# The opening of a one-layer decoder: zeros before the first rows, rows in half loads, a third tile's rows in a weight's place, and a new order where queries, keys and the feed-forward start

## The chip, the cores and the metric

The kernel runs on one core of one Trainium2 chip. A core has several engines that each work through their own instructions in order: TensorE (PE in the profile; its weight loads are PEld), VectorE (DVE), ScalarE (ACT), GpSimd (POOL) and SyncE (SP), which here issues the transfers (DMAs) between the memory of the device and the memory beside the engines. The engines wait for one another by semaphores. The metric is the device time of one execution in microseconds (us). The kernel before takes 2188.39 us, the median of 3 runs (2185.43 to 2188.78).

## The reference

One layer of a decoder, for a prompt of 2048 tokens and 64 sample tokens (8 sequences of 8), width 1024, all in 32-bit floats. Cut to what matters here:

```python
h = rms_norm(x, g_mix_pre)
proj = jnp.einsum('btd,de->bte', h, w_in)
q, k, v, gq, gk, gv, gr, glr = jnp.split(proj, points, axis=-1)
q, k = rope(q, pos), rope(k, pos)
attn = swa_banded(q, k, v, sinks)        # window of 128 tokens, 8 query heads, 2 key heads of 64
log_a = log_sigmoid(glr @ w_gk2 + b_gk) / 16
o, s_new = gla_chunked(gq, gk, gv, log_a, s_init)
gla_out = rms_norm(o, g_gla) * silu(gr)
x = x + rms_norm(concat([attn, gla_out]) @ w_out, g_mix_post)
u = relu(rms_norm(x, g_ffn_pre) @ w_up)  # 1024 -> 4096
x = x + rms_norm((u * u) @ w_down, g_ffn_post)
```

The sample tokens go through the same layer with a cache of keys and values and a state of the gated attention. Returned are the two outputs, the last windows of keys and values, and the states.

## The kernel before

**Numbers.** TensorE multiplies in a reduced 32-bit form, so each operand is split into a high part (written by ACT) and a low part (what is left, by DVE: source less high part), and each product is three: high by high, high by low, low by high. A name that ends in `h` or `_hi` is a high part, in `l` or `_lo` a low part. A helper class, `InOrder`, keeps the instructions that are recorded through `te`, `ac` and `dv` (TensorE, ScalarE, VectorE) in the order of the code; all of those carry line L131 in the profile. What goes through `nc.gpsimd` and `nc.sync` stands on POOL and SP in the order of the code as well. Nothing is put in order at run time.

**Stages.** The tokens are cut into tiles of 128 rows, 16 of the prompt and one of the samples.

1. *Opening* (`start`). The rows of tiles 0 and 1 (`x_0`, `x_1`) are loaded, turned by TensorE (`xT`: eight products of 128x128 with the identity, in two halves) and split (`xh`, `xl`). The 784 columns of `w_in` that make q, k, v and the gate's ranks come in 16 pieces (`wa_raw`) and are split too (`wa_hi`, `wa_lo`), with the gain column `gcol`. Then come the first column half of the projection for both tiles, the second half for tile 0, tile 2's rows in between, the second half for tile 1, and the first queries and keys.
2. *Attention* (loop `for i in range(NB)`). For each tile four units of scores (`sc`), turned probabilities (`pT`) and values (`av`). In between TensorE fills in the projection of later tiles (`fill`). A table, `A_PLAN`, says at which unit and phase the side work is done: the row norm of tile i+3 (`junk`, then `rstd`), the rotation of tile i+1, its turned queries and keys (`pq`, `pk`, in `heads_T`), and their splits (`qh`, `ql`, `kh`, `kl`; in the code `hi1`, `lo0`, `lo1`, `klo0`, `klo1`). From i = 3 on two pieces of the gate's weights (`wg`) are loaded and split per tile. At i = 4 in the code, `load_consts` makes the masks and `wgk`; those of its instructions that are not kept in order by the helper stand wherever their inputs and the scheduler put them.
3. *Gated attention*, then the *output projection* with the row norms that follow.
4. *Feed-forward*. The up projection is done with seven products for eight (sums of blocks, `H[p]` for the tokens' sums and `s13`, `s24` for the weights' sums). The tokens' sums are built per pair of tiles in a tile `ht` of seven rows and stored (`h_d`). The first block column is special (`opening(p, ...)`): its products are worked in the order `UP_FIRST` = 1, 0, 2, 8, 5, 7, 9, 6, 3, 4, where 0, 8 and 9 are steps of the sample tokens, and the last rows of the stage before are finished between them. The results (`uX`, `uc`, `ud`, `ue`, `ua`, `ub` in the profile, by the bank they lie in) are added into `st`.

**Where a transfer waits.** SP's transfers take eight semaphores in rotation; a tile that is written again waits until the readers of its old content are done, and a reader may be a store that has not landed.

Of the kernel before, what the change touches and what calls it, by code (L numbers as in the profile page):

```python
# [21 lines left out]
P = 128  # L22
# [34 lines left out]
A_LEAD = 14  # L57
A_PLAN = [(name, (int(at[0]), at[1])) for name, at in dict(
    klo0="3T", first="1B", hi1="3C", x1="1B", lo1="0A", klo1="0B", rest="3A", lo0="3A", junk="2A", turn="1A", rstd="1A", vl="3S", x0="1A"
# [57 lines left out]
def f32(ap):  # L117
    return ap.bitcast(F32)
# [23 lines left out]
def hybrid_step_kernel(ctx: ExitStack, tc: tile.TileContext, I, O):  # L142
# [100 lines left out]
    with nc.allow_non_contiguous_dma(reason="a column of gains"):  # L243
        nc.sync.dma_start(gcol, I["g_mix_pre"][0].rearrange("(k p) -> p k", p=P))

# [38 lines left out]
    def load_x(i):  # L284
        xs_in[i] = x = sp.tile([P, D], F32, tag="x", name=f"x_{i}", bufs=2)
        nc.sync.dma_start(x[: rows(i)], x_rows(i))
# [125 lines left out]
    def heads_T(i):  # L412
# [12 lines left out]
        pk = bank([P, P], "b", f"pk_{i}")  # L425
# [12 lines left out]
        for r in range(2):  # L438
# [10 lines left out]
        def k_lo(r):  # L449
            dv.tensor_tensor(kl[half_of[r], r, 1, :], pk[half_of[r]], f32(ks[half_of[r], r, 1, :]), op=ALU.subtract)  # L450
            nc.gpsimd.tensor_copy(kl[half_of[1 - r], r, 1, :], f32(kl[half_of[r], r, 1, :]))

        def q_lo(r):
# [4 lines left out]
        return {  # L458
            "klo0": lambda: k_lo(0),
# [182 lines left out]
    def load_consts():  # L642
# [12 lines left out]
        for u, rr in enumerate(half_of):  # L655
            nc.scalar.activation(wgk[rr, u], gk[rr], AF.Copy)
            lo = slice(u * HD + 32, u * HD + HD)
            nc.vector.tensor_tensor(gk[lo], gk[lo], f32(wgk[lo, u]), op=ALU.subtract)
            nc.vector.tensor_tensor(wgk[lo, u], gk[lo], extra[lo], op=ALU.add)
        at = [0]  # L660

        def part(n, shape, dtype):
# [3 lines left out]
            nc.vector.tensor_copy(t.rearrange("p a b -> p (a b)") if len(shape) > 1 else t, src)  # L666
# [9 lines left out]
        return wgk, msk, smsk, dmsk, onehot, ggla  # L676
# [9 lines left out]
    def start():  # L686
# [16 lines left out]
        load_x(0)  # L703
# [3 lines left out]
        load_x(1)  # L707
# [23 lines left out]
        for k in range(KT):  # L731
            split(1, k)
            run(second[0], 3)
        for norm in norms:
            norm()
# [1529 lines left out]
```

## Time and profile before

| what | number |
|---|---|
| median of 3 runs | 2188.39 us (2185.43 to 2188.78) |
| the profiled execution | 2189.12 us, its span 2187.3 us |
| TensorE busy | 2156.4 us, 99% of the span |
| DVE, ACT, POOL busy | 1530.3, 1221.7, 251.7 us |
| transfers | 411.54 MB, mean 188 GB/s |
| mean granted TensorE clock | 0.995 of full |

The span is the profiled part of one execution; the execution's own time is 1.8 us longer. In the lists of waits and of instructions a row names the tile that is written and the tiles that are read (`out<-in`), and in square brackets the time for which the engine was idle before it and what it had waited for. "PEclk" is the granted clock as a share of the full one. Matmuls overlap their successors, so the time from start to start of two rows is what TensorE needs, and the duration that a row shows is somewhat longer.

### The profile page before, as it was taken

The numbers are of one execution on the slowest core, as the hardware profiler recorded it, in microseconds if no ns is written. First come the engines' busy times: TensorE is split into PE (matmuls) and PEld (weight loads), VectorE is DVE, ScalarE is ACT, GpSimd is POOL, SyncE is SP. The second block draws the span as 40 slices with busy tenths as digits, with TensorE's granted clock in tenths as the row PEclk, the third lists the DMA queues.
The fourth block names the chain that finished last, engine by engine and source line by source line (L and its number), as shares of the span: only waits on it lengthen the run. The fifth ranks groups of instructions, "written<-read, shape, count | busy, mean of one in ns | idle before, by whom it ended". The sixth has DMA issues, their size and how long they took to land.

```text
span 2187.3 us, 34212 instructions
## 1 busy us (share of the span) xinstructions
PE 2156.4 (99%) x11784; PEld 1866.2 (85%) x11784; DVE 1530.3 (70%) x3203; ACT 1221.7 (56%) x2626; POOL 251.7 (12%) x410
## 2 busy tenths in 40 slices
PE   8999999999999999899999999999999999999998
PEld 7999999999998888788888887888888888888886
DVE  5999968777775666788888555548676666555566
ACT  5899867566663544555555544435444455444444
POOL 2567521111121100000000000000000000000000
PEclk9999999999999999999999999999999999999999
DMA  6444331224337666777876777758544443766685
GB/s 223 139 138 158 103 116 60 69 84 157 108 137 261 216 202 212 233 261 250 276 251 244 255 237 221 242 180 269 182 179 151 159 142 128 238 203 196 194 270 185
DMA packets 240314, 411.54 MB, mean 188 GB/s; under 512 B 25924, under 2 KB 142124, under 8 KB 236028
## 3 DMA queue, kind: packets, MB, share of 16 engines
q1 hardware_dynamic: 240140, 409.35, 56.5%
q8 instruction: 93, 1.52, 0.3%
q14 instruction: 81, 0.66, 0.1%
HBM read 265.82 MB, written 143.99 MB: 187 GB/s over the span
## 4 chain that ended last, share of the span: by engine, by line
PE 92%; DVE 3%; ACT 2%; DMA 1%; issue 1%; POOL 0%; SPq 0%; DVEq 0%; ACTq 0%; POOLq 0%
PE dn L131 27%; PE gproj L131 12%; PE uc L131 8%; PE uX L131 8%; PE out L1335 7%; PE proj L131 6%; PE ud L131 4%; PE ub L131 4%; PE ue L131 4%; PE sam L131 1%; PE dsam L131 1%; PE sc L131 1%; PE pT L131 1%; PE o L131 1%; PE av L131 1%; PE out L131 1%
## 5 line engine op out<-in xcount | busy, mean ns | idle before, releaser
L131 PE MATMUL dn<-o0t,o0s 128*128 128x512 f32 x896 | 349.3, 390 | 2.9 <-ACT o0t L219 1.3
L131 PE MATMUL dn<-o1t,o0s 128*128 128x512 f32 x896 | 349.6, 390 | 0.7 <-DVE o1t L220 0.7
L131 PE MATMUL dn<-o0t,o1s 128*128 128x512 f32 x896 | 349.3, 390 | 0.0
L220 DVE TENSOR_TENSOR o1s<-rs,o0s 128x512 fp32r<-128x512 f32 x224 | 154.6, 691 | 231.4 <-ACT o0s L219 226.6
L219 ACT ACTIVATE o0s<-rs 128x512 fp32r<-128x512 f32 x224 | 141.1, 631 | 305.4 <-PE dn L131 286.1
L131 PE MATMUL gproj<-wg,gxh 128*128 128x384 f32 x1024 | 272.6, 342 | 0.0
L131 PEld LDWEIGHTS dn<-o0t,o0s 128*128 128x128 f32 x896 | 168.2, 188 | 40.4 <-ACT o0t L219 2.1
L131 PEld LDWEIGHTS dn<-o1t,o0s 128*128 128x128 f32 x896 | 168.2, 188 | 37.9 <-DVE o1t L220 2.1
L131 PEld LDWEIGHTS dn<-o0t,o1s 128*128 128x128 f32 x896 | 168.2, 188 | 35.2
L131 ACT ACTIVATE st<-st 128x512 f32<-128x512 f32 x224 | 141.2, 630 | 99.6 <-DVE st L131 94.4
L131 PE MATMUL uc<-H,s 128*128 128x512 f32 x768 | 188.9, 395 | 2.8 <-ACT st L131 2.8
L131 PEld LDWEIGHTS gproj<-wg,gxh 128*128 128x128 f32 x1024 | 183.7, 188 | 3.5 <-issue 3.1
L131 PE MATMUL gproj<-wg,gxl 128*128 128x384 f32 x576 | 185.6, 340 | 0.0
L131 PE MATMUL uX<-H,w 128*128 128x512 f32 x768 | 185.6, 390 | 0.0
L131 PEld LDWEIGHTS uc<-H,s 128*128 128x128 f32 x768 | 144.6, 190 | 33.9 <-ACT st L131 3.0
L131 PEld LDWEIGHTS uX<-H,w 128*128 128x128 f32 x768 | 144.4, 188 | 30.6
L220 DVE TENSOR_TENSOR o1t<-rt,o0t 128x512 fp32r<-128x512 f32 x224 | 153.1, 684 | 9.4 <-ACT o0t L219 9.2
L1335 PE MATMUL out<-wo,mt 128*128 128x512 f32 x680 | 158.6, 392 | 0.0
L209 POOL TENSOR_TENSOR frs<-rs_v,half 128x1 f32<-128x1 f32 (+1 forms) x13 | 10.1, 786 | 1211.6 <-DVE rs_v L207 690.2
L1335 PEld LDWEIGHTS out<-wo,mt 128*128 128x128 f32 x680 | 126.5, 188 | 26.1
L219 ACT ACTIVATE o0t<-rt 128x512 fp32r<-128x512 f32 x224 | 138.1, 617 | 12.0 <-DMA rt<-t_d 8.8
L131 DVE TENSOR_TENSOR st<-st 128x512 f32<-128x512 f32 x160 | 110.6, 691 | 29.2 <-ACT st L131 25.0
(407 smaller groups left out, 4300.2 us busy)
## 6 DMA issues: line engine op xcount, KB each, us to landing
s_d<-st SPq DMA_DIRECT2D x32, 1792.0 KB, 8.5
rs<-s_d SPq DMA_DIRECT2D x224, 256.0 KB, 2.8
raw<-in_w_up SPq DMA_DIRECT2D x64, 512.0 KB, 4.4
rt<-t_d SPq DMA_DIRECT2D x128, 256.0 KB, 3.8
rt<-in_w_down SPq DMA_DIRECT2D x96, 256.0 KB, 3.2
t<-in_w_down SPq DMA_DIRECT2D x64, 256.0 KB, 3.9
t_d<-t SPq DMA_DIRECT2D x32, 512.0 KB, 3.2
hraw<-h_d SPq DMA_DIRECT2D x20, 512.0 KB, 4.9
```

Of the source, the lines that this page charges most:

```text
L131: ins = call(*a, **k)
L209: nc.gpsimd.tensor_tensor(out, v[:n], e, op=ALU.pow)
L219: nc.scalar.activation(hi, src, AF.Copy)
L220: vector.tensor_tensor(lo, src, f32(hi), op=ALU.subtract)
L1335: te.matmul(banks[c], x, w[:, c * 512 : (c + 1) * 512], start=k + u == 0, stop=k == KT - 1 and u == len(products) - 1,)
```

## The change

There are five parts.

1. *Zeros first.* TensorE multiplies a 128x128 tile of zeros by itself 16 times before anything else. The rows of tile 0 are loaded in two halves of their columns, the gain column's load moves behind them, the rotation tables (`rope`) of tiles 0 to 2 move behind the weights, and tile 2's rows are loaded earlier. The row norms of tiles 0 and 1 are done within the second column half's loop, and the stores of their turned rows are issued before that loop.
2. *Tile 2's rows* lie in the place of gate weight 1 (free until i = 3), so that splitting them no longer waits for the stores of tile 0's.
3. *First queries and keys first.* For tile 0 the turned keys get a bank of their own ("c"), the splits of its queries and keys stand ahead of tile 1's remaining columns, half of the key copies moves into the first unit, the row norm of tile 2 moves behind the first unit's scores, and DVE instead of POOL makes the second copies of `kl`. `A_OPEN` is a small table for what is left of this at i = 0.
4. *Constants and gate weights.* The arithmetic of `load_consts` becomes a step of the table (i = 4, unit 2, phase A) and half of it goes from DVE to POOL. At i = 3 the two gate weights are split at two units instead of one; at i = 15 the additional one moves from unit 2 to unit 3.
5. *Feed-forward opening.* The rows of tile 11 are copied to `ht` one step earlier; the second half of the tokens uses one `ht` tile for all four pairs, and its rows 0 and 1 are stored by themselves, ahead of the other five; the two loads of `H41`, `H40` change places; the additions, squares and splits around products 6, 3 and 4 change order; the low part of the next weight and the sum `s24` move; the last additions of the first block column move ahead of the next one's.

```diff
+    (name, (int(at[0]), at[1]))
+    for name, at in dict(kh1="0T", norm2="0S", rs2="0C").items()
+WARM = 16
...
-        nc.sync.dma_start(gcol, I["g_mix_pre"][0].rearrange("(k p) -> p k", p=P))
...
-        pk = bank([P, P], "b", f"pk_{i}")
+        pk = bank([P, P], "b" if i else "c", f"pk_{i}")
...
+        k_hi(0)
         if i > 0:
+            k_hi(1)
...
-            nc.gpsimd.tensor_copy(kl[half_of[1 - r], r, 1, :], f32(kl[half_of[r], r, 1, :]))
+            if i > 0:
+                nc.gpsimd.tensor_copy(kl[half_of[1 - r], r, 1, :], f32(kl[half_of[r], r, 1, :]))
+            else:
+                dv.tensor_tensor(kl[half_of[1 - r], r, 1, :], pk[half_of[r]], hi, op=ALU.subtract)
...
-            nc.scalar.activation(wgk[rr, u], gk[rr], AF.Copy)
-            lo = slice(u * HD + 32, u * HD + HD)
-            nc.vector.tensor_tensor(gk[lo], gk[lo], f32(wgk[lo, u]), op=ALU.subtract)
-            nc.vector.tensor_tensor(wgk[lo, u], gk[lo], extra[lo], op=ALU.add)
...
+        def make():
+            for u, rr in enumerate(half_of):
+                ac.activation(wgk[rr, u], gk[rr], AF.Copy)
+                lo = slice(u * HD + 32, u * HD + HD)
+                nc.gpsimd.tensor_tensor(gk[lo], gk[lo], f32(wgk[lo, u]), op=ALU.subtract)
+                nc.gpsimd.tensor_tensor(wgk[lo, u], gk[lo], extra[lo], op=ALU.add)
+            for copy in made:
+                dv.tensor_copy(*copy)
...
-        load_x(0)
+        warm = sp.tile([P, 2 * P], F32, tag="spc", name="warm", bufs=2)
+        nc.vector.memset(warm[:, :P], 0.0)
+        idle = bank([P, P], "e", "idle")
+        for _ in range(WARM):
+            te.matmul(idle, warm[:, :P], warm[:, :P], start=True, stop=True)
+        load_x(0, 2, rope=False)
...
-        for norm in norms:
-            norm()
+        load_x(2, rope=False)
+        for i in range(3):
+            load_rope(i)
...
+        store()
+        for k in range(KT):
+            split(1, k)
+            run(second[0], 3)
+            if k in (1, 3):
+                norms[k // 2]()
+        xTs[2] = [t[:, :, :P] for t in gw[G_EARLY[1]][1:]]
...
+        left = heads_T(0)
+        for name in ("hi1", "klo0", "lo0", "lo1"):
+            left.pop(name)()
         rest = take_rest(1)
         rest()
-        norm = x_norm(2)
         load_x(3)
-        store()
-        for left in heads_T(0).values():
-            left()
-        norm()
+        left["norm2"] = lambda: left.update(rs2=x_norm(2))
...
-                split_some(2)
+                split_some(1 if i == 3 else 2)
...
-                split_some(1 + (u == 2))
+                split_some(1 + (u == 3))
+            elif u == 2 and i == 3:
+                split_some(1)
...
+            for u in ((1, 0) if (sb, p) == (0, 4) else (0, 1))
...
-            sums[sb, j] = ht_place(f"ht_{i}")
+            sums[sb, j] = sums[sb, j - 1] if sb and j else ht_place(f"ht_{i}")
...
+            if i < NB and sb and i != B_ORDER[-2]:
+                nc.sync.dma_start(h_d[sb][:, :2, :, q], ht[:, :2])
             return
...
-        latest_store[:] = [nc.sync.dma_start(h_d[sb][:, kept, :, q], ht[:, kept])]
+        latest_store[:] = [nc.sync.dma_start(h_d[sb][:, 2:, :, q], ht[:, 2:])]
...
+def split_low(sb, fc, which, vector):
+        hi, lo = halves_[sb, fc, which]
+        vector.tensor_tensor(lo, raws[sb, fc][which], f32(hi), op=ALU.subtract)
...
-                deque(before, 0)
+                if fc > 1 or sb:
+                    deque(before, 0)
...
+            elif p == 5:
+                deque(before, 0)
...
         if p == 1:
+            for copy in late_copies:
+                ac.activation(*copy)
+            nc.sync.dma_start(h_d[1][:, :2, :, 3 * P :], sums[1, 3][:, :2])
             taken(p)
...
             ahead("a")
-            for copy in late_copies:
-                ac.activation(*copy)
...
             taken(p)
+            next(last_rows)
             next(last_rows)
...
             ahead("13")
+            ahead("s24")
             run(last_rows)
...
             up_product(0, 1, 1, next_X[0])
-            taken(p)
...
-            ahead("s24")
             ahead("24")
-            split_up(0, 1, 1, ac, dv)
+            split_up(0, 1, 1, ac, None)
+            taken(6)
+            add(6, 1, "Z")
+            split_low(0, 1, 1, dv)
+            add(1, 1, "V")
```

The change adds no matmul but the 16 of zeros. Two places show how the order on ScalarE moves.

The first is ScalarE at the end of the opening, from tile 1's first column half (`qk`) to the first scores (`s_0_0`). Before:

```order
L131 ACTIVATE qk_485<-proj_0_319,rstd_all 128x392
L131 ACTIVATE qk_485<-proj_1_454,rstd_all 128x248
L131 ACTIVATE glr<-proj_1_454,rstd_all 128x2x16
L131 ACTIVATE vv_489<-proj_1_454,rstd_all 128x2x64
L131 ACTIVATE junk_493,ssq_494<-x_425 128x1024
L131 ACTIVATE qh_513<-pq_506 64x512
L131 ACTIVATE kh_515<-pk_511 64x128 x4
L131 ACTIVATE ql_514<-pq_506 64x512
L131 ACTIVATE sinkp<-pj 128x2
L131 ACTIVATE s_0_0_551,den_0_0_567<-s_0_0_551,m_0_0_564 128x129 x2
```

Now, a few rows further (`xh_597` is the first half of tile 3's turned rows, `junk_605` the row norm of tile 2):

```order
L136 ACTIVATE qk_506<-proj_0_335,rstd_all 128x392
L136 ACTIVATE qh_516<-pq_509 64x512
L136 ACTIVATE kh_518<-pk_514 64x128 x2
L136 ACTIVATE ql_517<-pq_509 64x512
L136 ACTIVATE qk_506<-proj_1_475,rstd_all 128x248
L136 ACTIVATE glr<-proj_1_475,rstd_all 128x2x16
L136 ACTIVATE vv_530<-proj_1_475,rstd_all 128x2x64
L136 ACTIVATE sinkp<-pj 128x2
L136 ACTIVATE kh_518<-pk_514 64x128 x2
L136 ACTIVATE s_0_0_557,den_0_0_575<-s_0_0_557,m_0_0_570 128x129 x2
L136 ACTIVATE s_0_0_557<-s_0_0_557,den_0_0_575 128x128
L136 ACTIVATE xh_597<-xT_0_599 128x512
```

The queries' high part now stands directly behind tile 1's first columns, with half of the key copies, and `junk` has left this stretch: it is the row behind `xh_597`.

The second is ScalarE in the feed-forward's opening, from the sum for product 2 of the next block column (`s_0_1`) on. `st_0` collects the first block column's results, `st_1` the second's, `samq` and `samp` are the sample tokens', `w_0_1` is the next weight. Before:

```order
L131 ACTIVATE s_0_1_11147<-t_0_1_11109 128x1024
L131 ACTIVATE st_0_10978<-st_0_10978 128x512 x2
L131 ACTIVATE samq_11183<-sam_10998 128x128
L131 ACTIVATE st_0_10978<-st_0_10978 128x512 x2
L131 ACTIVATE s_0_1_11222<-t_0_1_11109 128x1024
L131 ACTIVATE w_0_1_11226<-raw_0_1_10974 128x1024
L131 ACTIVATE samq_11183<-samq_11183 128x128 x2
L131 ACTIVATE samp_11184<-samq_11183 128x2x64
L131 ACTIVATE st_0_10978<-st_0_10978 128x512 x2
L131 ACTIVATE st_1_11251<-uX_1_11166 128x512
L131 ACTIVATE st_1_11251<-uc_1_11238 128x512
```

Now:

```order
L136 ACTIVATE s_0_1_11166<-t_0_1_11130 128x1024
L136 ACTIVATE samq_11200<-sam_11016 128x128
L136 ACTIVATE s_0_1_11234<-t_0_1_11130 128x1024
L136 ACTIVATE w_0_1_11238<-raw_0_1_10992 128x1024
L136 ACTIVATE st_0_10996<-st_0_10996 128x512 x4
L136 ACTIVATE samq_11200<-samq_11200 128x128 x2
L136 ACTIVATE samp_11201<-samq_11200 128x2x64
L136 ACTIVATE st_1_11266<-uX_1_11187 128x512
L136 ACTIVATE st_1_11266<-uc_1_11258 128x512
L136 ACTIVATE st_0_10996<-st_0_10996 128x512 x2
```

The two squares of `st_0` that stood ahead of the second `s_0_1` and of `w_0_1` now stand behind them, and the last two, which stood ahead of the copies into `st_1`, now stand behind those. Some fifteen rows earlier the two copies `ht<-xnT` of tile 11 have moved from behind the first `w_0_1` to ahead of the first copy `st_0<-uX`.

More of the change, by code (lines that the diff above doesn't have):

```diff
@@ L57 @@
 A_LEAD = 14
+A_OPEN = [
+    (name, (int(at[0]), at[1]))
+    for name, at in dict(kh1="0T", norm2="0S", rs2="0C").items()
+]
+WARM = 16
 A_PLAN = [(name, (int(at[0]), at[1])) for name, at in dict(
-    klo0="3T", first="1B", hi1="3C", x1="1B", lo1="0A", klo1="0B", rest="3A", lo0="3A", junk="2A", turn="1A", rstd="1A", vl="3S", x0="1A"
+    klo0="3T", first="1B", hi1="3C", x1="1B", lo1="0A", klo1="0B", rest="3A", lo0="3A", junk="2A", turn="1A", rstd="1A", vl="3S", x0="1A", consts="2A"
 ).items()]
@@ L770, in start @@
         run(fill, A_LEAD)
+        return left
     def split_some(n):
@@ L783, in hybrid_step_kernel @@
     sink = None
-    start()
+    todo = start()
     kcs, cached = {}, {}
@@ L801, in hybrid_step_kernel @@
         next(unit_)
-    todo = {}
     for i in range(NB):
@@ L1471, in h_place @@
     def h_place(sb, p):
-        H[p] = [h_pools[p].tile([P, KT // 2, BT], F32R, tag=f"h{p}{u}", name=f"H{p}{u}_{sb}", bufs=1) for u in range(2)]
+        H[p] = [
+            h_pools[p].tile([P, KT // 2, BT], F32R, tag=f"h{p}{u}", name=f"H{p}{u}_{sb}", bufs=1)
+            for u in ((1, 0) if (sb, p) == (0, 4) else (0, 1))
+        ]
+        if (sb, p) == (0, 4):
+            H[p].reverse()
     def open_pools(to, names, label, side="left"):
@@ L1808, in up @@
                 sample_up(fc, p // 8, sam)
-            if p == 3:
+            if p == 3 and not first:
                 add(6, s(1), Z)
             if first:
-                opening(p, taken, ahead)
-                if p == 3:
+                opening(p, taken, ahead, lambda out, a, b: add(out, s(a), {"Z": Z, "V": V}[b]))
+                if p == 4:
                     squared(s(6))
@@ L1845, in end @@
         def end():
-            add(1, s(1), V)
+            if not first:
+                add(1, s(1), V)
             yield
@@ L1893, in opening @@
             taken(p)
-            next(last_rows)
             split_in_place(4)
```

46 lines of the change are left out of this document (26 added, 20 removed).

## The prediction

> **What bounds the kernel now.** I read the page first, then TensorE's waits, the granted clock by stretches, and the list of instructions where those two point.
>
> ```profile
> span 2187.3 us, 34212 instructions
> ...
> PE 2156.4 (99%) x11784; PEld 1866.2 (85%) x11784; DVE 1530.3 (70%) x3203; ACT 1221.7 (56%) x2626; POOL 251.7 (12%) x410
> ```
>
> TensorE is the bound, so only two things can be won without taking products away: time in which it waits, and time in which it multiplies at half its clock. Its waits, by what ended them (total, times, longest):
>
> ```profile
> PE xT L131 <- DMA x<-in_x_prompt: 6.0, 1, 6.0
> PE uc L131 <- ACT st L131: 2.8, 1, 2.8
> PE xnT L131 <- ACT ht L131: 1.6, 1, 1.6
> PE av L131 <- DVE pl L131: 1.5, 2, 1.1
> ```
>
> The waits lie in the first 120 us and around 880 to 915 us, the places that the change rewrites. The clock shows the second price (stretch, its length, busy time of PE, PEld, DVE, ACT, POOL, granted clock, DMA share, GB/s):
>
> ```profile
> 34.00:37.00 3.00, 0.41 (x3) 0.25 (x2) 2.05 (x5) 0.87 (x3) 2.80 (x6) 0.94 0.80 262
> 37.00:42.00 5.00, 5.00 (x17) 4.90 (x17) 1.21 (x8) 1.33 (x5) 3.18 (x6) 0.50 0.36 98
> 42.00:44.00 2.00, 2.00 (x13) 2.00 (x12) 0.28 (x1) 0.61 (x2) 0.00 (x0) 0.63 0.09 17
> 914.00:920.00 6.00, 5.41 (x13) 4.25 (x14) 5.38 (x8) 2.81 (x5) 0.00 (x0) 0.50 0.95 380
> ```
>
> Behind the gaps near 35 and 913 us the clock is half for some 6.8 us (the share lost in the first three rows is 3.00 x 0.06 + 5.00 x 0.50 + 2.00 x 0.37 = 3.4 us, half of 6.8). So a gap of 2.6 to 2.8 us costs 6, not 2.7; this is where most of the change's price must come from.
>
> **Opening, up to the second tile's projection: -0.3 us.** From the chain of waits (first row), the order of time on DVE (second) and on TensorE:
>
> ```profile
> 1.24 4.60 DMA x<-in_x_prompt
> ```
> ```profile
> 0.81 0.06 DVE L196 MEMSET half<- 128x1 f32 x1 [0.81 <-PEq L2253]
> ```
> ```profile
> 5.97 1.94 PE L131 MATMUL xT<-ident,x 128*128 128x128 f32 x8 [5.97 <-DMA x<-in_x_prompt]
> ...
> 13.10 1.03 PE L131 MATMUL xT<-ident,x 128*128 128x128 f32 x8
> 14.38 0.99 PE L131 MATMUL proj<-wa_hi,xh 128*128 128x392 f32 x4 [0.25 <-ACT xh L131]
> ...
> 30.99 0.38 PE L131 MATMUL pj<-sinkj,sel 4*128 4x2 f32 x2
> ```
>
> The clock's record says full from the start, but eight turns take 1.94 us at 5.97 and 1.03 us at 13.10: TensorE starts at half speed. The zeros can begin when DVE has cleared the tile, about 1.2 us. `pj` is one plain 32-bit product in the code and two instructions in the trace, so 16 zeros products are 32 passes of 128 columns, at about 0.21 us cold (1.94 over 8, less the pipeline's tail) 6.8 us, at 0.11 warm 3.5 us. If all are cold they end at 8.0; the rows, which land in halves before the 5.84 us of the whole load (1.24 + 4.60), then wait for the zeros instead of the reverse. From the first turn to tile 1's first product the kernel before needs 14.38 - 5.97 = 8.4 us, of which I take off 1.5 for the full clock (0.5 of the turns, about 1.0 of the projection, whose other limits are the splits on ACT and DVE): 6.9. So 8.0 + 6.9 = 14.9 against 14.38, a loss of 0.5; with the clock up in mid-way (end at 7.0) a gain of 0.5; the bounds are a gain of 1.1 (zeros at half speed for one half of a cold phase, end at 6.4) and a loss of 1.3 (half clock stays another 1.6 us behind the zeros). I take the middle, -0.3, since the second half of the 6.8 us phase may lie in front of or behind their end. The moved loads (gain column, rotation tables, tile 2), the earlier stores and the norms inside the second loop I cost at nothing: TensorE's list has no gap from 14.38 to 33.9, so its products hide them, and ACT has idle time there (1.15 us ahead of the row at 27.45 below); were that cover gone, each `junk` (1.06 us, below) would show.
>
> [...]
>
> **First queries and keys, tile 0: +5.2 us.** The turned queries of each tile (`pq`) mark the period; two scores (`sc`) wait:
>
> ```profile
> 30.35 0.60 PE L131 MATMUL pq<-ident,rot 128*128 128x128 f32 x4
> ...
> 35.28 0.30 PE L131 MATMUL sc<-kh,qh 128*128 128x128 f32 x1 [1.22 <-DVE qh L131]
> 36.94 0.47 PE L131 MATMUL sc<-kl,qh 128*128 128x128 f32 x1 [1.36 <-POOL kl L451]
> ...
> 49.65 0.60 PE L131 MATMUL pq<-ident,rot 128*128 128x128 f32 x4
> ...
> 67.72 0.60 PE L131 MATMUL pq<-ident,rot 128*128 128x128 f32 x4
> ...
> 83.56 0.60 PE L131 MATMUL pq<-ident,rot 128*128 128x128 f32 x4
> ...
> 99.43 0.60 PE L131 MATMUL pq<-ident,rot 128*128 128x128 f32 x4
> ...
> 116.25 0.60 PE L131 MATMUL pq<-ident,rot 128*128 128x128 f32 x4
> ```
> ```profile
> 27.45 1.09 ACT L131 ACTIVATE xh<-xT 128x512 fp32r<-128x512 f32 x2 [1.15 <-DMA xt_d<-xh]
> ...
> 31.45 1.06 ACT L131 ACTIVATE junk<-x 128x1024 bf16<-128x1024 f32 x1
> ...
> 110.68 1.11 ACT L131 ACTIVATE wg<-wg_raw,gcol 128x384 fp32r<-128x384 f32 x2
> ```
>
> The first period is 49.65 - 30.35 = 19.3 us: 2.6 of waits (1.22 + 1.36), 3.4 of half clock, and 13.3 of work. In the new order the queries' high part no longer stands behind tile 1's rest, `junk` (1.06) and four key copies, so about 2 us of ACT leave the path to `sc`, and `kl`'s second copy is DVE's instead of POOL's, which was busy with tile 1's rotation. Tile 2's place in the gate weight takes the 1.15 us out that ACT waits for the store there, so the splits of tile 2 are no longer late either. Both waits go, and with them the half clock. What is late next: the norm of tile 2. DVE's part of it now stands behind the first unit's scores and waits for `junk`, which on ACT stands behind tile 3's first half; behind it on DVE stand tile 3's low half, the next scores and `pl`, for which `av` waits. I count 1.1 us there, one `junk`; 6.0 - 1.1 and 0.3 of pipeline tails give 5.2. Bounds: 4.0 (the wait is twice that) and 6.3 (none).
>
> **Tile 1 and the constants: +1.8 and +0.5 us.** The second period is 67.72 - 49.65 = 18.1 against 83.56 to 99.43 = 15.9 undisturbed. In it DVE spends
>
> ```profile
> 54.12 1.15 DVE L658 TENSOR_TENSOR c_raw<-c_raw,wgk 32x256 f32<-32x256 f32 x1
> ...
> 56.09 1.83 DVE L659 TENSOR_TENSOR wgk<-c_raw 32x256 fp32r<-32x256 f32 x1
> ```
> ```profile
> 59.23 0.33 PE L131 MATMUL av<-pl,vv 128*64 128x256 f32 x1 [1.12 <-DVE pl L131]
> ```
>
> on constants that the change takes to POOL and to a later tile. 2.2 is the whole excess; I take 1.8 (1.0 to 2.3). The period from 99.43 to 116.25 is 16.8, 0.9 more than its neighbour, with both gate weights split in one go (`wg` at 110.68); spreading them wins up to 0.9, and the constants, now ACT and DVE work at i = 4, cost from nothing (ACT is 56% busy) to 0.8: +0.5 (-0.3 to 0.9), the changed unit at i = 15 included.
>
> **Feed-forward opening: +8.8 us.** On TensorE, and in the chain:
>
> ```profile
> 880.26 2.91 PE L131 MATMUL uc<-H,s 128*128 128x512 f32 x12
> 884.74 1.14 PE L131 MATMUL xnT<-ident,x 128*128 128x128 f32 x8 [1.57 <-ACT ht L131]
> ...
> 899.74 2.90 PE L131 MATMUL uc<-H,s 128*128 128x512 f32 x12
> 902.48 2.88 PE L131 MATMUL ue<-H,s 128*128 128x512 f32 x12
> 905.19 1.11 PE L131 MATMUL sam<-w,xsT 128*128 128x256 f32 x8
> ...
> 914.59 5.49 PE L131 MATMUL uc<-H,s 128*128 128x512 f32 x12 [2.78 <-ACT st L131]
> ...
> 925.98 2.20 PE L131 MATMUL uX<-H,w 128*128 128x512 f32 x9
> ```
> ```profile
> 874.34 9.73 DMA h_d<-ht
> ...
> 890.33 5.64 DMA H<-h_d
> ```
>
> From 880.26 to 925.98 are 45.7 us with twelve products. One takes 902.48 - 899.74 = 2.74; 12 x 2.74 + 0.9 (`xnT`) + 2.2 (two `sam`, about 1.0 each, and two turns) = 36.0. So 9.7 are lost: 5.6 of waits, the rest at half clock (`uc` takes 5.49). The chain says why: tile 11's copies to `ht` wait for the store of its old content (9.73), then `H` for its load (5.64), then the sums, squares and copies on DVE and ACT one behind the other, up to the copy that frees `uc`'s bank. In the new order rows 0 and 1 have landed by themselves, so the copies run at about 875 and `xnT` at 883 does not wait; the load of `H41` stands on SP behind one more store but some 4 us earlier, at about 886; `s24` and the next weight are split ahead of the squares. What is late next: the copy of `uX` into `st_1` waits for the last store of rows 2 to 6, issued at about 900. With 1280 of the 1792 KB its landing takes 5/7 of 9.73 = 6.9 us, 907; TensorE comes to that `uc` at 908. I take off 0.9 for a rest of wait: 8.8. Bounds: 9.7, and 6.0 with a store that takes the whole 9.73 (wait of 2.9, clock kept).
>
> **Sum.** -0.3 + 5.2 + 1.8 + 0.5 + 8.8 = 16.0 us, against the profiled execution: 2189.12 - 16.0 = 2173.1. It lies 0.7 above the median of the three runs, so against the median 2172.4; I say 2172.5. By the terms' bounds 9.4 to 20.3.
>
> **Rivals.**
> [...]
> (b) *The store wins in the feed-forward.* If the last store takes its 9.73 us, or more because the next loads share its queue, `uc` waits 2.9 and, as at 912, the clock halves: 2.9 + 3.4 = 6.3 return: 2178.7.
> (c) *The norm takes the place of the queries.* If `av` waits over 2 us in the first unit, in a stretch with another gap, the half clock stays: the term falls to about 1: 2177.
> (d) *The head start is given back.* If a later stage waits on a transfer with less slack than 7 us, 7.2 are lost: 2180. Against it: beside the first rows, no wait of TensorE in the list is put down to a transfer.
> (e) *Slower: one `ht` tile for four pairs.* In the output projection the three later pairs rewrite rows 0 and 1, and then the other five, of a tile whose stores may still be under way: six places for a wait. Each gap of 2.8 us costs 6.2 with the clock, as at 912. Three of them eat the gain (18.6, 2191), from four on it is slower (2197). TensorE's products there are
>
> ```profile
> L1335 PE MATMUL out<-wo,mt 128*128 128x512 f32 x680 | 158.6, 392 | 0.0
> ```
>
> 158.6 / 17 = 9.3 us a tile, so about 20 us a pair with the turns, against 9.73 for the longest store: a landing would have to double before it decides.
>
> **How the numbers follow.** 0.2%, 4.4 us, is about what a measurement of this kernel tells from no change. Forecast 0.50; (a) 0.12, (b) 0.11, (c) 0.09, (d) 0.04, (e) 0.14, of which 0.04 for two or three gaps (2185 to 2191, within 0.2%). Faster are the forecast and (a) to (d), 0.86; same 0.04; slower 0.10. The low end is the sum's best bound and a little more, 2166; the high end takes in (b) and (c) together (6.3 + 4.2 returned, 2183). Only (e) and tails are outside.
>
> **What would show it.** Right: TensorE's first instruction near 1.2 us and `xT` near 8 with no wait for `x`; `pq` to `pq` 14 us, then 16.5; granted clock 1.00 from 34 to 44 us and through the up projection's first 50 us; `av` the largest wait of the first 60 us; `xnT` without a wait; twelve products in about 37 us. Wrong: a clock of 0.50 in either place (then the gap in front of it names the rival), `xT` later than 9, or a wait on `h_d<-ht` before 870 us. I would be most wrong if a stretch that I called covered turned out to have no slack on DVE.

## The result, and the profile after

The changed kernel takes 2173.41 us, the median of 6 runs (2172.02 to 2175.46), the kernel before 2187.89 us in the same runs (6 runs, 2185.43 to 2188.78). The ratio is 0.9936 (95% interval 0.9924 to 0.9949). The forecast was 2172.5 us, with a range of 2166 to 2183.

The page of the changed kernel:

```profile
span 2171.2 us, 34290 instructions
...
PE 2152.2 (99%) x11816; PEld 1865.2 (86%) x11816; DVE 1526.1 (70%) x3202; ACT 1219.4 (56%) x2626; POOL 254.1 (12%) x412
```

The span is 16.1 us shorter. TensorE has 32 instructions more, the 16 products of zeros. Its list of waits no longer holds the rows of tile 0, nor `uc`, nor the `xnT` of the feed-forward opening. Of the scores' waits it still has

```profile
PE sc L136 <- POOL kl L465: 1.1, 2, 0.6
```

The granted clock (the last but two of the columns) is full where it was half:

```profile
34.00:37.00 3.00, 3.00 (x22) 2.96 (x21) 1.85 (x11) 1.40 (x6) 2.92 (x4) 1.00 0.02 5
37.00:42.00 5.00, 4.03 (x31) 3.71 (x29) 2.59 (x13) 3.77 (x11) 4.21 (x8) 1.00 0.49 136
...
908.00:914.00 6.00, 6.00 (x28) 4.94 (x27) 4.24 (x6) 4.57 (x8) 0.00 (x0) 1.00 0.53 187
914.00:920.00 6.00, 6.00 (x32) 5.13 (x31) 4.77 (x9) 4.13 (x8) 0.00 (x0) 1.00 0.15 31
```

TensorE in order of time, at the start, with the one wait left at the first queries, the marks of the periods and the feed-forward's opening:

```profile
1.09 6.04 PE L136 MATMUL idle<-warm 128*128 128x128 f32 x32 [1.09 <-DVE warm L726]
6.97 1.04 PE L136 MATMUL xT<-ident,x 128*128 128x128 f32 x8
...
14.00 0.99 PE L136 MATMUL proj<-wa_hi,xh 128*128 128x392 f32 x4 [0.25 <-ACT xh L136]
...
29.96 0.60 PE L136 MATMUL pq<-ident,rot 128*128 128x128 f32 x4
...
40.35 0.33 PE L136 MATMUL av<-pl,vv 128*64 128x256 f32 x1 [0.97 <-DVE pl L136]
...
44.22 0.60 PE L136 MATMUL pq<-ident,rot 128*128 128x128 f32 x4
...
59.10 0.60 PE L136 MATMUL pq<-ident,rot 128*128 128x128 f32 x4
...
90.80 0.60 PE L136 MATMUL pq<-ident,rot 128*128 128x128 f32 x4
...
108.14 0.60 PE L136 MATMUL pq<-ident,rot 128*128 128x128 f32 x4
...
112.48 0.45 PE L136 MATMUL av<-pl,vv 128*64 128x256 f32 x2 [0.31 <-DVE pl L136]
114.12 0.39 PE L136 MATMUL sc<-kl,qh 128*128 128x256 f32 x1 [0.48 <-POOL kl L465]
...
125.49 0.60 PE L136 MATMUL pq<-ident,rot 128*128 128x128 f32 x4
...
873.98 2.92 PE L136 MATMUL uc<-H,s 128*128 128x512 f32 x12
876.73 1.03 PE L136 MATMUL xnT<-ident,x 128*128 128x128 f32 x8
...
898.09 2.91 PE L136 MATMUL ub<-H,s 128*128 128x512 f32 x12
...
910.30 2.88 PE L136 MATMUL uX<-H,w 128*128 128x512 f32 x12
```

The kernel before has its sixth and seventh `pq` at 116.25 and

```profile
132.26 0.60 PE L131 MATMUL pq<-ident,rot 128*128 128x128 f32 x4
```

Marks of the same work in both traces say where the 16.1 us went:

| stretch | before, us | after, us | won | forecast (bounds) |
|---|---|---|---|---|
| start to the first `pq` | 30.35 | 29.96 | 0.4 | -0.3 (-1.3 to 1.1) |
| first to second `pq` | 19.30 | 14.26 | 5.0 | 5.2 (4.0 to 6.3) |
| second to third `pq` | 18.07 | 14.88 | 3.2 | 1.8 (1.0 to 2.3) |
| third `pq` to `uc` in the feed-forward (880.26 and 873.98) | 812.54 | 814.88 | -2.3 | 0.5 (-0.3 to 0.9) |
| from there to the `uX` behind the opening (925.98 and 910.30) | 45.72 | 36.32 | 9.4 | 8.8 (6.0 to 9.7) |
| the rest of the span | 1261.3 | 1260.9 | 0.4 | 0 |

Three of the five forecast terms lie within their bounds. Two do not: the stretch with the constants and gate weights lost 2.3 us instead of winning 0.5, and tile 1's period won 3.2 instead of 1.8, which takes back half of that error. Of the 2.3 us, 1.9 lie in the fifth and sixth periods (17.34 and 17.35 us; 16.82 and 16.01 before), where the change put this work; 0.7 lie in the tenth, with a wait for `kl` of 0.57 us near 178 us whose cause stays open; the rest of the stretch wins 0.3 back.

### The profile page after: what moved, and what is told of

It is laid out like the page before. It is cut to its first block, busy times and chain, and to the rows that moved or that the text cites. A ratio compares the mean times of both kernels' runs of the same rounds, so it can differ in the third digit from the quotient of the medians.

```text
span 2171.2 us, 34290 instructions
## 1 busy us (share of the span) xinstructions
PE 2152.2 (99%) x11816; PEld 1865.2 (86%) x11816; DVE 1526.1 (70%) x3202; ACT 1219.4 (56%) x2626; POOL 254.1 (12%) x412
## 4 chain that ended last, share of the span: by engine, by line
PE 94%; ACT 2%; DMA 1%; DVE 1%; issue 1%; POOL 0%; SPq 0%; DVEq 0%; ACTq 0%; POOLq 0%
PE dn L136 27%; PE gproj L136 13%; PE uc L136 8%; PE uX L136 8%; PE out L1369 7%; PE proj L136 6%; PE ud L136 4%; PE ub L136 4%; PE ue L136 4%; PE sam L136 2%; PE dsam L136 1%; PE o L136 1%; PE sc L136 1%; PE pT L136 1%; PE av L136 1%; PE gl L136 1%
```

## The experiments

### Do the parts add up?

`head_only` is the kernel before with parts 1 to 4, `ff_only` the kernel before with part 5. Their edits are the change's diff, cut at the feed-forward.

> The kernel before with parts 1 to 4 of the change and without part 5 (the feed-forward opening). If the parts simply add up: the distance from the first feed-forward product before the stall (uc) to uX behind it stays 45.7 us, with a wait of about 2.8 us and a granted clock of 0.50 behind it, and the time is 2187.9 less the 6.3 us that the changed kernel has won by its first feed-forward product: about 2181 to 2182. If the head start is instead swallowed by transfers in front of the feed-forward (rival d), the time stays at 2185 or more.

> The kernel before with part 5 alone. If the parts add up: 2187.9 - 9.4 = about 2178.5, with the stretch of twelve products at 36 to 37 us and a granted clock of 1.00 from 914 to 922 us; the two waits of the scores near 35 us and the half clock behind them stay. If the feed-forward opening only profits because the head start gives its loads more time, the stretch stays over 40 us and the time over 2182.

`head_only` took 2182.66 us (ratio to before 0.9973, 0.9963 to 0.9982), `ff_only` 2178.22 us (0.9956, 0.9941 to 0.9971). Against the 2188.44 us of before in these runs the parts win 5.8 and 10.2 us, 16.0 together; the whole change won 14.5. They add up within what the runs can tell (1.5 us, where the runs of one kernel lie 2 to 6 us apart), so the head start is not swallowed in front of the feed-forward (rival d), and the feed-forward does not live on it.

Two things were not expected. In `head_only` the same copies and squares keep TensorE waiting as before, but the stretch from `uc` to the `uX` behind the opening is 42.9 us (873.81 to 916.70), not 45.7:

```profile
878.95 1.14 PE L136 MATMUL xnT<-ident,x 128*128 128x128 f32 x8 [2.22 <-ACT ht L136]
...
908.12 3.04 PE L136 MATMUL uc<-H,s 128*128 128x512 f32 x12 [2.39 <-ACT st L136]
```

The twelve passes of `uc` take 3.04 us and not 5.49: behind a wait of 2.39 us the clock stayed full, while behind 2.78 us before it had halved. In the same profile the shorter wait of 2.22 us was followed by half clock (`ud` takes 4.59 us there). And in `ff_only`, where the two waits of the first scores stand as they were (1.23 and 1.29 us),

```profile
34.00:37.00 3.00, 0.48 (x3) 0.34 (x2) 2.08 (x5) 0.84 (x3) 2.73 (x6) 0.95 0.87 268
37.00:42.00 5.00, 5.00 (x25) 4.96 (x26) 1.18 (x8) 1.61 (x6) 3.14 (x6) 0.69 0.35 99
```

1.7 us are lost to the half clock (3.00 x 0.05 + 5.00 x 0.31) where the profile before has 3.4. So the same gap costs sometimes more and sometimes less through the clock.

### The zeros

`no_zeros` leaves out the zeros, `zeros8` halves them:

```diff
-        warm = sp.tile([P, 2 * P], F32, tag="spc", name="warm", bufs=2)
-        nc.vector.memset(warm[:, :P], 0.0)
-        idle = bank([P, P], "e", "idle")
-        for _ in range(WARM):
-            te.matmul(idle, warm[:, :P], warm[:, :P], start=True, stop=True)
```
```diff
-WARM = 16
+WARM = 8
```

> The changed kernel without the 16 products of zeros; the rows of tile 0 still come in halves. My prediction's step (zeros cost about what the warm clock saves): the rows land near 5.3 us, TensorE starts cold there, tile 1's first product comes at 13.4 to 14.3 us (14.00 with zeros) and the time stays within 0.7 us of 2173.4. Rival (the warm start is worth more than the wait for the zeros' end): first product at 15.0 us or later, time 2174.5 or more.

> The changed kernel with 8 products of zeros instead of 16: 16 cold passes end near 4.5 us, then TensorE waits until the rows land near 5.3. [...]

Without zeros the time is 2174.21 us (2170.06 to 2175.94), with eight 2174.36 (2171.88 to 2174.8), with sixteen 2173.41: no difference that the runs can tell. The two cases of the expectation without zeros lie about 1 us apart, which is less than the runs of one kernel differ. Without zeros the rows land at 3.75, not at the 5.3 that I had taken:

```profile
3.75 1.94 PE L136 MATMUL xT<-ident,x 128*128 128x128 f32 x8 [3.75 <-DMA x<-in_x_prompt]
...
13.03 0.98 PE L136 MATMUL proj<-wa_hi,xh 128*128 128x392 f32 x4 [0.25 <-ACT xh L136]
```

Sixteen zeros thus hold the rows back by 3.2 us (6.97 against 3.75) and win 2.2 of them back by the clock. In this execution the kernel without them was 1.0 us ahead at tile 1's first product (13.03 against 14.00), but the other two profiles without zeros (`mended_no_zeros` and `apart` below, which have this opening) have it at 14.58 and 13.71 us: one waits longer for the first weights (1.94 us against 1.31), and in both the clock comes up later (the second turns take 1.71 and 1.42 us, here 1.03). The rows' new place in the queue and their halves, not the zeros, replaced the wait of 6 us.

Eight zeros show the clock at work:

```profile
1.09 3.78 PE L136 MATMUL idle<-warm 128*128 128x128 f32 x16 [1.09 <-DVE warm L726]
4.67 1.20 PE L136 MATMUL xT<-ident,x 128*128 128x128 f32 x8
6.82 0.96 PE L136 MATMUL proj<-wa_hi,xh 128*128 128x392 f32 x2 [0.95 <-ACT wa_hi L136]
8.52 1.23 PE L136 MATMUL proj<-wa_hi,xh 128*128 128x392 f32 x2 [0.73 <-ACT wa_hi L136]
9.54 1.51 PE L136 MATMUL proj<-wa_lo,xh 128*128 128x392 f32 x4
...
12.01 1.03 PE L136 MATMUL xT<-ident,x 128*128 128x128 f32 x8
13.30 0.99 PE L136 MATMUL proj<-wa_hi,xh 128*128 128x392 f32 x4 [0.25 <-ACT xh L136]
```

The turns take 1.20 us, mostly full clock (1.94 us at half speed and 1.03 at full in the kernel before); behind the two gaps of 0.95 and 0.73 us the products are slow again (four take 1.51 us; with 16 zeros, behind gaps of 0.76 and 0.55 us, 1.11), and by 12 us they are fast (eight turns in 1.03 us). The zeros end about where they were expected (the turns begin at 4.67 us, near the 4.5), but the rows are there by then, not at 5.3; the clock came up early, and fell again within the opening.

### The first queries and keys

`queries_old` puts the old order back at the end of the opening, with tile 2's new place and DVE's second copies of `kl`:

```diff
-        left = heads_T(0)
-        for name in ("hi1", "klo0", "lo0", "lo1"):
-            left.pop(name)()
         rest = take_rest(1)
         rest()
         load_x(3)
-        left["norm2"] = lambda: left.update(rs2=x_norm(2))
+        left = {"rs2": x_norm(2)}
+        for part in heads_T(0).values():
+            part()
```

> The changed kernel with the old order at the end of the opening: tile 1's remaining columns, tile 2's norm (junk) and all four key copies stand around the queries' high part again; tile 2's rows stay in the gate weight's place, and DVE still makes the second copies of kl. My step for the first queries and keys (the order on ACT keeps the scores waiting): the first scores wait 1.2 to 1.8 us for the queries' low part, the wait of 0.97 us at av goes, and the period from the first pq to the second is 14.5 to 15.5 us instead of 14.26; if the wait also halves the clock, 17 or more. Rival (tile 2's place alone removed the waits, the order did nothing): no wait of the scores over 0.3 us, period 13.3.

2174.23 us (2173.76 to 2176.41). The first period is 15.08 us (pq at 29.72 and 44.80), and one wait of the scores is back, as expected, with the clock full:

```profile
34.84 0.30 PE L136 MATMUL sc<-kh,qh 128*128 128x128 f32 x1 [1.42 <-DVE qh L136]
```

The order on ACT does what the step said, but it is worth 0.8 us (15.08 - 14.26), since its gain of 1.4 is paid with 0.97 at `av`. The larger part of the 5.0 us, 4.2, was won by what this kernel keeps: the second wait (for `kl` from POOL) is gone, and one wait of 1.4 us alone did not halve the clock here, where two of 1.2 and 1.4 us had. How much of the 4.2 is the clock's depends on the execution: in `ff_only`, with the old order and the same two waits, the first period took 17.78 us and not 19.30. Which of the two kept edits (tile 2's place, DVE's copies) did it was not tried apart.

### The feed-forward opening

`ff_rows_old` undoes the early rows, `ff_order_old` the order of the sums and squares:

```diff
-            sums[sb, j] = sums[sb, j - 1] if sb and j else ht_place(f"ht_{i}")
+            sums[sb, j] = ht_place(f"ht_{i}")
...
-        latest_store[:] = [nc.sync.dma_start(h_d[sb][:, 2:, :, q], ht[:, 2:])]
+        latest_store[:] = [nc.sync.dma_start(h_d[sb][:, kept, :, q], ht[:, kept])]
...
         elif p == 2:
             taken(p)
             ahead("a")
+            for copy in late_copies:
+                ac.activation(*copy)
```
```diff
         elif p == 6:
             next_X.append(bank([P, BT], "a", "uX_0_1"))
             up_product(0, 1, 1, next_X[0])
+            taken(p)
...
         else:
+            ahead("s24")
             ahead("24")
-            split_up(0, 1, 1, ac, None)
-            taken(6)
-            add(6, 1, "Z")
-            split_low(0, 1, 1, dv)
-            add(1, 1, "V")
+            split_up(0, 1, 1, ac, dv)
```

> The changed kernel with the rows in the feed-forward opening as before: one store of all seven rows per pair, a tile of its own for each pair, the copies of tile 11 behind the first next weight. The order of sums and squares stays new. My step (the late copies start the chain): xnT waits 1.5 to 2.2 us again, the load of H41 starts some 4 us later, and a second wait of 1 us or more stands at ub or uc; time 2176 to 2179. Rival (the order of the squares did it): only the wait at xnT comes back, time 2175 or less.

> The changed kernel with the old order of sums, squares and splits around products 6, 3 and 4 in the feed-forward opening; the early rows, the split stores and H41 first stay new. My step (both belong to one chain, the rows start it 4 us earlier): xnT does not wait; at ub and uc together 0 to 1.5 us of waits, clock full, time 2173.5 to 2175.5. Rival (the order is what counts): the wait of 2 us or more at uc stays, time 2176 or more.

`ff_rows_old` took 2178.71 us (2177.79 to 2180.34):

```profile
878.67 1.15 PE L136 MATMUL xnT<-ident,x 128*128 128x128 f32 x8 [2.17 <-ACT ht L136]
879.57 4.58 PE L136 MATMUL ud<-H,s 128*128 128x512 f32 x12
```
```profile
905.76 3.03 PE L136 MATMUL uc<-H,s 128*128 128x512 f32 x12 [0.30 <-ACT st L136]
```

The wait at `xnT` is back, with a half clock behind it (`ud` takes 4.58 us instead of 3.02), but the late wait is 0.30 us only: the time is the one that the step gave, the waits are those of the rival. `ff_order_old` took 2179.55 us (2178.74 to 2181.38):

```profile
890.20 2.79 PE L136 MATMUL ud<-H,w 128*128 128x512 f32 x11 [0.59 <-DVE H L136]
900.02 0.73 PE L136 MATMUL ub<-H,s 128*128 128x512 f32 x2 [0.62 <-ACT s L136]
901.28 2.58 PE L136 MATMUL ub<-H,s 128*128 128x512 f32 x10 [0.53 <-DVE s L136]
907.56 4.62 PE L136 MATMUL uc<-H,s 128*128 128x512 f32 x12 [2.76 <-ACT st L136]
```

Here `xnT` does not wait, and the late waits are all there, 4.5 us of them and a half clock, as the rival said. So each edit removes a stall that the other does not. By the medians the rows are worth 5.3 us (2178.71 - 2173.41) and the order 6.1. By the marks the stretch from `uc` to the `uX` behind the opening is 40.75 us with the old rows (873.58 to 914.33) and 43.51 with the old order (874.25 to 917.76), against 36.32: 4.4 and 7.2 us, 11.6 together, where both at once win 9.4. The two stalls are thus not independent. One tie between them is ScalarE's copy of `uX`, which stands ahead of the copy that frees `uc`'s bank and waits for the last store, first in the changed kernel, then in `ff_rows_old`:

```profile
900.59 0.60 ACT L136 ACTIVATE st<-uX 128x512 f32<-128x512 f32 x1 [0.98 <-DMA h_d<-ht]
```
```profile
904.62 0.60 ACT L136 ACTIVATE st<-uX 128x512 f32<-128x512 f32 x1 [3.06 <-DMA h_d<-ht]
```

With the old rows the store lands 4.0 us later. TensorE, held up at `xnT`, is late by as much (it comes to `uc` 32.2 us after the stretch's first product, and 27.8 in the changed kernel), and so only 0.30 us of the late wait shows. My step expected the early rows to shorten the late waits by their 4 us; with the old order they shortened them by nothing: 4.5 us, against 2.4 in `head_only`, where TensorE is held up at `xnT` first.

### The constants and the gate weights

`three` tries three repairs at once, `mended` is the same with the other choice at two of them. First `three`:

```diff
-    for name, at in dict(kh1="0T", norm2="0S", rs2="0C").items()
+    for name, at in dict(kh1="0T", norm2="0A", rs2="0C").items()
...
+        if i == 2:
+            wgk, msk, smsk, dmsk, onehot, ggla, todo["consts"] = load_consts()
         if i == 4:
...
-            wgk, msk, smsk, dmsk, onehot, ggla, todo["consts"] = load_consts()
...
-                split_some(1 if i == 3 else 2)
+                split_some(1 if i == 4 else 2)
...
-            elif u == 2 and i == 3:
+            elif u == 2 and i == 4:
```

> The changed kernel with three repairs: tile 2's norm stands at phase A of the first unit instead of S (ahead of tile 3's first half on ACT), the constants are loaded and made at i = 2 instead of 4 (GpSimd has no gate weight to prepare there), and the gate weights that are spread over two units are those of i = 4 instead of i = 3. From the changed kernel's rows: av's wait of 0.97 us goes, the waits of 0.42 (pT), 0.31 (av) and 0.48 us (sc for kl) between 105 and 115 us go, so the pq periods there are 13.3 after the first and 15.9 to 16.2 at i = 3 and 4 instead of 17.3; the time is 2 to 3 us less than the changed kernel's, about 2171. Rival: GpSimd is late there for another reason (the gate weights themselves), the waits for kl stay, and only 1 us is won.

2175.08 us (2170.6 to 2175.57), nothing won that the runs can tell; from the first `pq` to the last the profile is 1.0 us shorter. The first period is 13.08 us (pq at 30.66 and 43.74): moving the norm took the wait at `av` away. But the fourth period, in which the constants now are made, is 17.31 us (74.52 to 91.83). The weights spread at i = 4 make the fifth 16.32 (91.83 to 108.15; 16.82 before) and the sixth 17.72 (108.15 to 125.87), where

```profile
113.46 0.45 PE L136 MATMUL av<-pl,vv 128*64 128x256 f32 x2 [1.42 <-DVE pl L136]
```

So spreading a pair of weights moves its second half to unit 2, where DVE and ACT split the next tile's queries and keys, and that costs more than it wins (1.7 us of the sixth period for 0.5 of the fifth). `mended` keeps the norm at phase A, goes back to both weights at unit 1 and puts the constants where no weights are left:

```diff
+        if i == NB - 5:
             wgk, msk, smsk, dmsk, onehot, ggla, todo["consts"] = load_consts()
...
-                split_some(1 if i == 3 else 2)
+                split_some(2)
...
-            elif u == 2 and i == 3:
-                split_some(1)
```

> The changed kernel with three repairs chosen from the traces so far: tile 2's norm at phase A of the first unit, both gate weights of i = 3 split at unit 1 again as before the change, and the constants loaded and made at i = 11, when no gate weight is left to prepare. Theory (each of the three places has its own term): periods from pq to pq of 13.1 (first; 14.26 in the changed kernel), 16.8 (fifth; 17.34), 16.0 (sixth; 17.35) and no new excess at i = 11 or 12 (15.9); the eighth pq 3.0 us earlier relative to the first one; time about 2170.5. Rival (the constants cost about 1.4 us wherever they stand, since ACT and DVE have no slack in this loop): a period of 17 or more at i = 11, and 1.5 us won in all.

2171.08 us (2170.33 to 2174.36; ratio to before 0.9925, 0.9913 to 0.9938). The marks:

```profile
89.65 0.60 PE L136 MATMUL pq<-ident,rot 128*128 128x128 f32 x4
...
106.48 0.60 PE L136 MATMUL pq<-ident,rot 128*128 128x128 f32 x4
...
122.54 0.60 PE L136 MATMUL pq<-ident,rot 128*128 128x128 f32 x4
...
217.89 0.60 PE L136 MATMUL pq<-ident,rot 128*128 128x128 f32 x4
...
222.06 0.45 PE L136 MATMUL av<-pl,vv 128*64 128x256 f32 x2 [0.30 <-DVE pl L136]
223.84 0.38 PE L136 MATMUL sc<-kl,qh 128*128 128x256 f32 x1 [0.61 <-POOL kl L465]
...
235.22 0.60 PE L136 MATMUL pq<-ident,rot 128*128 128x128 f32 x4
```

Fifth period 16.83 (17.34 in the changed kernel, 16.82 before): the change's spreading at i = 3 cost 0.5. Sixth 16.06 (17.35): free of the constants. And 17.33 where the constants are now: they cost about 1.4 us at i = 2, at 4 and at 11 alike, with the same two waits, for `pl` from DVE and `kl` from POOL. Part of their arithmetic now stands on POOL, and whether DVE, ACT or POOL sets this price was not tried apart. The theory of a free place at i = 11 fell, and its rival held; what `mended` wins, 2.2 us up to the last `pq` by the marks, is the norm's 1.0 to 1.2, the spreading's 0.5, and a wait for `kl` near 178 us (0.57) that the changed kernel's profile has and this one has not.

### The zeros once more, and a clock that falls behind narrow products

> The same without the 16 products of zeros. Theory (from the kernel without zeros: the rows land at 3.75 us, the zeros end at 7): the first pq comes at about 29.0 instead of 29.7 to 30.7, all later ones keep their distances, and the time is about 1 us less than with zeros, 2169.5. Rival (the zeros pay): no difference or longer.

`mended_no_zeros` (both edits above) took 2173.51 us (2171.94 to 2175.8) against 2171.08 with zeros: the theory fell, no gain. In both comparisons, this one and the one above, the kernel with zeros has the lower median (by 2.4 and 0.8 us), with runs that overlap; whether the zeros are worth something stays open. Its first `pq` is at 30.52, not 29.0, after a wait of 1.94 us for the first weights.

The runs of most of these kernels lie 2 to 6 us apart, and the profiles show a place that differs between executions. In `mended`, 380 to 388 us:

```profile
380.00:388.00 8.00, 8.00 (x93) 7.09 (x92) 4.91 (x13) 2.67 (x9) 0.00 (x0) 0.79 0.39 134
```

TensorE counts as busy throughout, and yet the clock is granted at 0.79. The same is in six of the ten profiles that have this order there and the new head (0.67 to 0.79), and not in the other four, the changed kernel's among them, nor in the two with the old head (`before` and `ff_only`). Ahead of it stand

```profile
378.17 1.10 PE L136 MATMUL s_oi<-s_at,gp_s 64*128 64x64 f32 x8
379.20 1.96 PE L136 MATMUL s_oe<-s_qz,s 128*128 128x16 f32 x16
```

sample-token passes of 64 and of 16 columns. `apart` sets them apart, on top of `mended_no_zeros`; `best` does it the other way round on top of `mended`:

```diff
         yield
-        yield
         oi = bank([P, 4, NS], "b", "s_oi")
...
         nc.scalar.activation(s_oT, oi, AF.Copy)
+        yield
         for g in range(2):
```
```diff
-S_WAIT = (2, 6)
+S_WAIT = (2, 5)
...
         nc.scalar.activation(s_oT, oi, AF.Copy)
+        yield
         for g in range(2):
```

> The kernel without zeros and with the three repairs, and in the gated attention the sample tokens' narrow products are set apart: the eight passes of 64 columns (s_oi) one step earlier than the sixteen of 16 columns (s_oe), with projection products between. Theory (these 3 us of narrow products, which the profile counts as busy, let the clock fall to half in some executions and not in others): no half clock between 380 and 390 us, the spread of the runs shrinks to 3 us or less, the median falls by 1 to 2 us. Rival (the half clock there has another cause): granted clock under 1.00 between 380 and 390 us in the profile, or a spread of 5 us as before.

> The changed kernel with zeros, with the three repairs, and with the sixteen narrow passes (s_oe) one step later than the eight before them (s_oi), instead of the eight one step earlier: projection products stand between, and one of the later idle steps of the sample tokens is dropped. Theory: no wait at s_oi (0.9 us in the kernel that moved it forward), granted clock 1.00 from 380 to 390 us, a median of about 2170 and runs within 3 us. Rival (the spread of the runs comes from elsewhere too): clock 1.00 there but runs 4 us apart, median 2171 as without this edit.

`apart`: 2172.28 us, 2171.79 to 2172.80 in five runs, and

```profile
380.00:388.00 8.00, 8.00 (x104) 7.16 (x103) 5.41 (x16) 2.28 (x9) 0.00 (x0) 1.00 0.42 135
```

The spread is 1.0 us instead of 3.9, the median 1.2 us lower, although `s_oi` now waits 0.9 us for DVE. `best` has no such wait and the clock at 1.00 there too, but its median is 2171.22 (2170.6 to 2174.34; ratio to before 0.9927, 0.9913 to 0.994), no better than `mended`, and its runs lie 3.7 us apart: in the profiled one the down projection waits 2.4 us for DVE and 1.5 for ACT (the tile `f`), against 1.3 and 0.7 in the changed kernel. So the spread has other sources too. That the narrow products are one of them is not shown: two profiles without half clock may be chance where six of twelve have none, and of the two kernels that set them apart only one has a small spread.

## Why the prediction was right, and where not

- **What bounds the kernel.** Right: the gain is waits and half clock, at the two places read from the list of waits, and the parts add up.
- **The sum.** 16.0 us forecast, 16.1 by the marks and 14.5 by the medians. That it is so close is in part luck: the rows of the table missed by +0.7, -0.2, +1.4, -2.8, +0.6 and +0.4 us, and these cancel.
- **Opening.** Within its bounds, 0.7 us better than said. The zeros ended at 7.0 us, not at 8.0; for an end at 7.0 the prediction had a gain of 0.5, and tile 1's first product came 0.4 earlier (14.00 against 14.38). For the start with zeros the bounds take the 6.8 us of half speed seen near 40 us, or half of that; no run shows either there. With 16 zeros the 32 passes took 5.9 us from start to start, which at 0.21 cold and 0.11 warm (both estimated from the turns) needs the full clock from about 6 us on, 5 us after the first pass; with 8 zeros, by an estimate from the turns' 1.20 us, it was up about 4 us after it. Nor does a run show what the 0.12 of (a) rests on; these two starts, and a gain of 0.4, are what the runs showed. It is a matter of 1 us, and the rows landed early enough (3.75 us without zeros) that the runs cannot tell whether the zeros pay.
- **First queries and keys.** Right in size, and the forecast wait at `av` came (1.1 forecast, 0.97 measured). The weight was put on the order on ACT, which is worth 0.8; most of the term is the second wait and the clock, and the clock's share (3.4 us in the profile that the forecast was read from, 1.7 in `ff_only`) is one execution's.
- **Tile 1 and the constants.** This is the step that failed, though it left the time within its range. It compared 18.1 us with the later periods' 15.9 and called 2.2 the whole excess; but this period has less work (105 matmul instructions against 112 in the next; 14.88 and 14.90 us in the kernels without constants in it), so the excess was 3.2. And it let the constants cost nothing to 0.8 us elsewhere, because ACT is 56% busy over the kernel; in this loop, by the stretch of the kernel before

```profile
100.00:150.00 50.00, 49.57 (x340) 47.77 (x339) 45.44 (x155) 45.79 (x125) 33.11 (x58) 1.00 0.50 168
```

DVE and ACT are busy for 45 and 46 of 50 us, and the constants cost 1.4 wherever they were put. A stretch without slack on DVE is what the prediction had named as the way to be most wrong. The spreading was credited with up to 0.9 for the pair at 110.68, but it spreads the pair of i = 3, and that pair lies at i = 4: the wait of 0.42 us at `pT` stayed, and unit 2 lost 0.5.
- **Feed-forward opening.** Right in size (8.8 against 9.4). The last store behaved as forecast: it is issued at 893.61 us, ACT's copy waits for it until 900.59 (7.0 us; 6.9 forecast), and TensorE comes to `uc` 1.2 us later and does not wait. Wrong in part of the mechanism: the late stall does not follow from the late rows alone, since with the old order it stayed when the rows were early.
- **Rivals.** None of (b) to (e) came: `uc` and the scores do not wait over 0.6 us, and between 700 and 850 us, in the output projection, TensorE idles 0.3 us.

## What to carry to other kernels

Read a stage's undisturbed period from that stage, not from its neighbour, and the slack of an engine from the loop into which work is moved: an average of 56% hid a loop at 90%. When a chain of waits names one path, undo its parts one at a time before calling it one cause, and compare the sum of what they are worth apart with what they win together. And before moving half of a burst to a quieter place, look up in the trace which burst the edit really moves, and what the engines do at the new place.

## What the runs showed of the hardware

- A gap's price through the clock varied from one profile to the next. Behind 1.2 + 1.4 us of waits the half clock cost 3.4 us in one (`before`), behind 1.2 + 1.3 us 1.7 in another (`ff_only`); behind waits of 2.78 (`before`) and 2.76 us (`ff_order_old`) `uc` took 5.49 and 4.62 us, behind 2.39 us (`head_only`) its usual 3.0.
- Short gaps did harm: 2.17 us (`ff_rows_old`, the twelve passes behind it in 4.58 us instead of 3.02), 2.22 us (`head_only`, 4.59), 2.76 us (`ff_order_old`, 4.62), and 0.95 + 0.73 us close together (`zeros8`, four products in 1.51 us instead of 0.88) were each followed by half clock.
- Half clock came although the profile shows no gap: 3 us of passes of 64 and 16 columns stood ahead of one in six of twelve profiles (mean granted clock 0.67 to 0.79 from 380 to 388 us, 1.00 from 380 to 400 us in the other six), and in neither of the two in which they were set apart (1.00). That they are the cause is not shown.
